# A hybrid retention and RG-LRU block: row factors squared earlier in the first steps, and all weight sums and rotary adds on VectorE

## The chip, the cores and the metric

The kernel runs on one core of a Trainium2 chip. The metric is the device time of one execution in microseconds (us); of the kernel before, three runs gave 929.69 us as the median (928.82 to 929.72). All arithmetic is float32; a product is split into high and low parts of the type fp32r and takes three matmuls.

The engines are named as in the profile: PE is TensorE, PEld its weight loads, DVE VectorE, ACT ScalarE, POOL GpSimd, SP the engine that issues most loads. Each engine executes its own instructions in order.

## The reference

One layer over 528 tokens (16 meta tokens ahead of 512) of width 1024:

```python
u = rmsnorm(h, mix_norm_w)
q, k, v, g_ret, lru_in, lru_gate, gate_a, gate_b = split(u @ w_in)      # 8 times 1024 columns
q, k = rotary(q), rotary(k) * 128 ** -0.5                               # 8 heads of 128
o = normed(chunk_retention(q, k, v))                                    # chunks of 128
y_ret = (silu(g_ret) * o) @ w_branch_ret
r = rg_lru(causal_depthwise_conv(lru_in))
y_lru = (gelu(lru_gate) * r) @ w_branch_lru
h = h + (sigmoid(gate_a) * y_ret + sigmoid(gate_b) * y_lru) @ w_out
u = rmsnorm(h, ffn_norm_w); g, up = split(u @ w_ffn_in)                 # 2 times 2816 columns
h = h + (silu(g) * up) @ w_ffn_out
out = rmsnorm(h, final_norm_w)[16:]
```

## The kernel before

The weights come in slabs of 2048 columns per partition, each in four quarters (`a21`, `a22`, `a11`, `a12`) of 128x512, loaded by SP into eight buffers (`raw`). `emit` (L268) prepares a quarter: ACT casts it to its high part (`hi`, L295), DVE subtracts that for the low part (`lo`, L299). A ring of nine high and low parts lies ahead of TensorE, and `weights` prepares up to eight pieces beyond the one asked for.

A slab is multiplied in one of two ways. `plain` (L439) uses the four quarters as they are. `fast` (L382) does with seven products what takes eight: it needs four sums of quarters (`s1` to `s4`, by `combine`, L260), sums of activations (`sums_of`, L531), and some adds of the products. Inside `fast`, DVE adds two products (`pz`, L398) after the first four blocks; the next block of TensorE writes the bank that this add reads, so TensorE can't go on before it. Of `w_in`, 13 slabs are fast, among them queries 0 to 3, keys 2, gates and LRU inputs; half of the values (`w_v`) is fast as well. Where `SUMS_ON_POOL` names the weights, `combine` puts the sums on POOL; for the FFN's `w_fi` they are on DVE. The queries and keys then go through `rotate` (L707): ACT copies halves, DVE multiplies by the tables (L720 or L716, and L721), POOL adds (L722).

The program order after the first steps is the order of the source, with other work deferred behind a count of TensorE time (`defer`, `tick`): retention, the convolution, the recurrence. The compiler's planner sets the order of each engine from it by a timeline of its own. The first steps are different: `first_steps` (L847) runs the list `FIRST_STEPS` (L47) in a section whose order on PE, DVE, ACT and POOL is kept as written; the planner may put later instructions between.

In that list, `f`, `h`, `l` weigh and split a token tile of 128 rows (first digit) and half of the width (second digit); `H` and `L` split a quarter of the value weights; `v` goes on with `plain_values` (L792) to the products of the next step: the first half of the width for tiles 0 and 1, the second half for tiles 0 and 1, then tile 2 (here called the third products), and, in a step behind the list, tile 3 (the fourth). `q` (`row_factor`, L593) squares a token tile's rows with a sum on ACT (L599), raises the mean to -0.5 on POOL (L602, L603) and puts the factor on a diagonal (L605). For tiles 2 and 3, `T` (`halve`) transposes the rows on TensorE by that diagonal into the bank `uT`; `x`, `h`, `l` weigh and split the result. For tiles 0 and 1 and the meta rows, whose transposed rows are loaded, `b` (`across`, L607) spreads the factors over all partitions by a product with ones, into the bank `rb`. `um` (`norm_meta`, L643) normalises the meta rows with DVE and ACT. `e01` evicts the products of tiles 0 and 1 from their banks, and `n`, `g`, `j` scale and split those tiles with the spread factors.

Of the kernel before, what the change touches and what calls it, by code (L numbers as in the profile page):

```python
# [14 lines left out]
ALU = mybir.AluOpType  # L15
# [29 lines left out]


FIRST_STEPS = ("f01 h01 H l01 L f00 H h00 L l00 H L H L v f11 h11 f10 h10 l11 l10 v H L H L H L H L v "  # L47
               "q2 qm q3 T21 T20 x21 h21 l21 x20 h20 l20 v q0 q1 T31 T30 bm b0 b1 x31 h31 l31 x30 h30 l30 um v "
               "e01 n00 g00 n01 g01 j00 j01 n10 g10 n11 g11 j10 j11").split()
STAGES = (3.5, 3.5, 9.0)  # L50
OUT = 14.0
BEGIN = 11.0
# [1 line left out]
LAST_K = 4  # L54

ON_POOL = {"w_out": (1, 3)}
SUMS_ON_POOL = ("w_in", "w_v")
Z_POOL = False
C_POOL = ()
STEPS = (2.0, 2.0, 1.0, 2.0)  # L60
# [51 lines left out]
class Slots:  # L112
# [12 lines left out]
    def get(self, n=SEQ, dt=F32):  # L125
        if n <= T and dt == F32:
            if self.halves:
                slot, i = self.halves.pop(0)
            else:
                slot, i = [*self.open(dt), 0], 0  # L130
                self.halves.append((slot, 1))
            slot[2] += 1
            t = slot[1][:, i * T:i * T + n]
            self.held[id(t)] = (t, slot, i)
        else:
            tag, mem = self.open(dt)
            t = mem[:, :n]
            self.held[id(t)] = (t, tag, None)
        return t

    def put(self, *tiles):
        for t in tiles:
            _, slot, i = self.held.pop(id(t))
            if i is None:
                self.free.append(slot)
                continue
            slot[2] -= 1
            self.halves.append((slot, i))
            if slot[2] == 0:
                self.halves = [h for h in self.halves if h[0] is not slot]  # L150
                self.free.append(slot[0])
# [3 lines left out]
def hybrid_block(ctx: ExitStack, tc: tile.TileContext, a: dict):  # L155
    nc = tc.nc
# [42 lines left out]
    for step in PLAN.split():  # L199
# [5 lines left out]
        else:  # L205
            key, base = SLAB_OF[step[0]]
# [7 lines left out]
    def on_pool(key, i, c):  # L214
        return c in ON_POOL.get(key, ())
# [23 lines left out]
    state = {"n": 0, "look": 0}  # L239

    def behind(ins, other):

        if other is not None:
            tc.add_manual_dep(ins.ins, other.ins.name, mybir.DependencyInfo(
                mybir.DependencyClass.NoSync, mybir.DependencyReason.DATA), reason="issue order")
        return ins
# [4 lines left out]
    sums = {}  # L251

    def quarter(key, i, c, queue=None):

        if (key, i, c) not in raws:
            raws[key, i, c] = wpool.tile([P, Q4], F32, tag="raw", bufs=RAW, name=f"raw_{key}{i}_{c}")
            (queue or nc.sync).dma_start(raws[key, i, c], a[key][i][:, c * Q4:(c + 1) * Q4])
        return raws[key, i, c]

    def combine(key, i, name, x, y, op):  # L260
        sums[key, i, name] = wpool.tile([P, Q4], F32, tag="sum", bufs=SUMS, name=f"{name}_{key}{i}")
        if key in SUMS_ON_POOL:
            behind(nc.gpsimd.tensor_tensor(sums[key, i, name], x, y, op=op), state.get("diag"))
        else:
            nc.vector.tensor_tensor(sums[key, i, name], x, y, op=op)
        return sums[key, i, name]

    def emit(n, later=False):  # L268
        key, i, c = pieces[n]
        a21, a22, a11, a12 = (lambda q=q: quarter(key, i, q) for q in range(4))  # L270
        apart = key == "w_v"
        if apart and c == "s1":
            t = kept[key, i] = sums[key, i, "s1"] = get()
            nc.gpsimd.tensor_tensor(t, a21(), a22(), op=ALU.add)
        elif apart and c == "s3":
            combine(key, i, "s3", a11(), a21(), ALU.subtract)
        elif apart and c in ("s2", "s4"):
            t = kept[key, i]
            if (key, i, "s2") not in sums:
                sums[key, i, "s2"] = t  # L280
                nc.gpsimd.tensor_tensor(t, t, a11(), op=ALU.subtract)
            if c == "s4":
                combine(key, i, "s4", a12(), t, ALU.subtract)
        elif c == "s1":
            s1 = combine(key, i, "s1", a21(), a22(), ALU.add)
            combine(key, i, "s3", a11(), a21(), ALU.subtract)
            s2 = combine(key, i, "s2", s1, a11(), ALU.subtract)
            combine(key, i, "s4", a12(), s2, ALU.subtract)
        if c in ("s1", "s2", "s3", "s4"):
            src = sums[key, i, c]  # L290
        else:
            src = quarter(key, i, {"a21": 0, "a22": 1, "a11": 2, "a12": 3}.get(c, c))
        hi = wpool.tile([P, Q4], F32R, tag="hi", bufs=RING, name=f"hi{n}")
        lo = wpool.tile([P, Q4], F32R, tag="lo", bufs=RING, name=f"lo{n}")
        nc.scalar.copy(hi, src)  # L295
        loaded[pieces[n]] = hi, lo

        def low(engine):
            engine.tensor_tensor(lo, src, hi.bitcast(F32), op=ALU.subtract)  # L299

        if later:
            return low
        low(nc.gpsimd if on_pool(key, i, c) else nc.vector)
        if (key, i) in kept and (key, i, "s4") in sums and {(key, i, "s2"), (key, i, "s4")} <= set(pieces[:n + 1]):
            put(kept.pop((key, i)))

    def advance(name):

        first = pieces.index(name)
        while state["n"] < min(first + RING, len(pieces)):  # L310
            emit(state["n"])
            state["n"] += 1

    def weights(*names):

        first, last = pieces.index(names[0]), pieces.index(names[-1])
        while state["n"] < min(max(last + state["look"], first) + 1, first + RING, len(pieces)):
            emit(state["n"])
            state["n"] += 1
        return [loaded.pop(n) for n in names]  # L320
# [231 lines left out]
    for load in FIRST_LOADS.split():  # L552
        t = int(load[1:] or 0)
        if load[0] == "w":
            key, i, c = pieces[t]
# [151 lines left out]
    def rotate(x, n, banks=()):  # L707

        tmp = get(4 * n)
        t = tmp.rearrange("p (j n t) -> p j n t", j=2, n=2)  # L710
        table = lambda r: rope[:, r, :, :n].unsqueeze(1).broadcast_to([P, 2, 2, n])
        for j, hs, pb in banks:
            pb = pb.rearrange("p (h t) -> p h t", t=n)
            nc.scalar.copy(t[:64, j, hs], pb[64:])
            nc.scalar.copy(t[64:, j, hs], pb[:64])
            nc.vector.tensor_tensor(x[:, j, hs], pb, rope[:, 0, hs, :n], op=ALU.mult)  # L716
        if not banks:
            nc.scalar.copy(t[:64], x[64:])
            nc.scalar.copy(t[64:], x[:64])
            nc.vector.tensor_tensor(x, x, table(0), op=ALU.mult)  # L720
        nc.vector.tensor_tensor(t, t, table(1), op=ALU.mult)  # L721
        nc.gpsimd.tensor_tensor(x, x, t, op=ALU.add)  # L722
        put(tmp)

    def value_block(out, w, x, h, start, tiles=(0, 1)):
# [121 lines left out]
    def first_steps(v):  # L847
        lows, parts = [], {}
        for step in FIRST_STEPS:
            kind, t, c = step[0], step[1:2], step[2:3]  # L850
            if step in ("v", "e01"):
                next(v, None)
            elif kind == "H":
                lows.append(emit(state["n"], True))
                state["n"] += 1
            elif kind == "L":
                lows.pop(0)(nc.vector)
            elif step == "um":
                norm_meta()
            elif kind == "q":  # L860
                row_factor(t if t == "m" else int(t))
            elif kind == "T":
                halve(int(t), int(c))
            elif kind == "x" or kind in "hl" and int(t) > 1:
                next(halves[int(t), int(c)], None)
            elif kind == "b":
                across(t if t == "m" else int(t))
            else:
                t, c = int(t), int(c)
                if kind == "n":  # L870
                    parts[t, c] = scaled(t, c)
                elif kind == "g":
                    nc.scalar.copy(parts[t, c][1][0], parts[t, c][0])
                elif kind == "j":
                    f, (hi, lo) = parts.pop((t, c))
                    nc.vector.tensor_tensor(lo, f, hi.bitcast(F32), op=ALU.subtract)
                else:
                    {"f": weighted, "h": raw_high, "l": raw_low}[kind](t, c)
# [362 lines left out]
    for hf in range(2):  # L1241
# [4 lines left out]
        for t, i in steps:  # L1246
# [5 lines left out]
            if i == KT - 1:  # L1252
                y = h_sb[t][:, hf * 512:(hf + 1) * 512]
# [191 lines left out]
```

## Time and profile before

| | us |
|---|---|
| median of three runs | 929.69 |
| the profiled execution | 928.09 |
| its span | 926.3 |
| PE busy | 907.6 |
| DVE busy | 659.3 |
| ACT busy | 462.6 |
| POOL busy | 177.3 |

The span runs from the first to the last instruction of the program; 1.8 us of the execution lie outside. Busy times are sums over an engine; TensorE's ends are modelled, and its matmuls overlap by a part. A row of a group gives line, engine, operation, output and inputs, shape and count, then busy us and mean ns, then the idle time ahead of it and what ended it. A row of a timeline gives start and duration in us; a row of a stretch gives its length and each engine's busy time in it.

### The profile page before, as it was taken

Reading aid. Unit: us, or ns where it says so; the run is one execution under the profiler, and the core shown is the slowest. Engines: PE = TensorE matmul, PEld = TensorE weight load, DVE = VectorE, ACT = ScalarE, POOL = GpSimd, SP = SyncE. Lnnn points to the kernel's source line nnn. Section 1 sums busy time; section 2 is a strip of 40 time slices with the busy share of each in tenths; the row PEclk is TensorE's granted clock in tenths of the full one; section 3 lists DMA queues with packets and bytes.
Section 4 is the critical chain, followed back from the end, with each engine's and each line's share of the span. In section 5 each row is a group of like instructions: output and inputs, shape, how many; then the busy total and the mean of one; then the engine's idle time right before and its main releaser. Section 6 shows DMA issues by size and latency. Waiting matters only on the chain.

```text
span 926.3 us, 16867 instructions
## 1 busy us (share of the span) xinstructions
PE 907.6 (98%) x6572; PEld 855.2 (92%) x6572; DVE 659.3 (71%) x1014; ACT 462.6 (50%) x815; POOL 177.3 (19%) x149
## 2 busy tenths in 40 slices
PE   8999999999999999999999999999999999999996
PEld 7899999999999889999998888999999999888885
DVE  5898986997788836787744536969999998832222
ACT  5654544653555337747932315545556566632213
POOL 2344553455351002112100212000000000000003
PEclk9999999999999999999999999999999999999999
DMA  9222122141133332232442222223333233432202
GB/s 327 80 95 91 58 81 92 58 126 46 60 111 115 110 100 76 91 109 88 148 136 91 93 91 76 81 79 120 104 106 120 96 123 96 151 111 91 80 1 91
DMA packets 49071, 92.59 MB, mean 100 GB/s; under 512 B 5584, under 2 KB 5840, under 8 KB 48992
## 3 DMA queue, kind: packets, MB, share of 16 engines
q1 hardware_dynamic: 47408, 87.55, 29.2%
q10 hardware_dynamic: 1584, 3.97, 1.3%
q8 instruction: 51, 0.84, 0.4%
q14 instruction: 28, 0.23, 0.1%
HBM read 89.40 MB, written 2.10 MB: 99 GB/s over the span
## 4 chain that ended last, share of the span: by engine, by line
PE 85%; DVE 3%; issue 1%; ACT 0%; POOLq 0%; POOL 0%; DVEq 0%
PE fo L369 4%; PE fo L368 4%; PE fo L367 4%; PE zwf L378 4%; PE zwf L377 4%; PE zwf L379 4%; PE yxf L378 3%; PE yxf L379 3%; PE yxf L377 3%; PE lg L377 2%; PE gate L377 2%; PE gate L379 2%; PE lg L379 2%; PE gate L378 2%; PE lg L378 2%; PE wo L367 2%
## 5 line engine op out<-in xcount | busy, mean ns | idle before, releaser
L299 DVE TENSOR_TENSOR lo<-raw_w_in,hi 128x512 fp32r<-128x512 f32 x99 | 85.2, 867 | 29.8 <-ACT hi L295 29.6
L295 ACT CAST hi<-raw_w_in 128x512 fp32r<-128x512 f32 x99 | 60.8, 619 | 62.7 <-PE w_br L368 13.9
L378 PE MATMUL zwf<-b,hi 128*128 128x256 f32 x304 | 84.7, 279 | 0.0
L379 PE MATMUL zwf<-b,lo 128*128 128x256 f32 x304 | 84.6, 278 | 0.0
L377 PE MATMUL zwf<-b,hi 128*128 128x256 f32 x304 | 84.5, 279 | 0.0
L299 DVE TENSOR_TENSOR lo<-raw_w_fo,hi 128x512 fp32r<-128x512 f32 x44 | 30.1, 690 | 63.3 <-ACT hi L295 63.3
L295 ACT CAST hi<-s_w_fi 128x512 fp32r<-128x512 f32 x76 | 47.2, 623 | 44.5 <-PE zwf L378 36.0
L368 PE MATMUL fo<-lo,b 128*128 128x512 f32 x176 | 69.3, 394 | 0.0
L367 PE MATMUL fo<-hi,b 128*128 128x512 f32 x176 | 69.3, 394 | 0.0
L369 PE MATMUL fo<-hi,b 128*128 128x512 f32 x176 | 69.3, 395 | 0.0
L1330 POOL TENSOR_TENSOR b<-b,b 128x512 f32<-128x512 f32 x4 | 5.1, 1287 | 330.0 <-ACT b L1329 330.0
L378 PE MATMUL yxf<-b,hi 128*128 128x256 f32 x228 | 62.8, 279 | 0.0
L379 PE MATMUL yxf<-b,lo 128*128 128x256 f32 x228 | 62.7, 278 | 0.0
L295 ACT CAST hi<-raw_w_fo 128x512 fp32r<-128x512 f32 x44 | 27.3, 620 | 70.2 <-PE fo L369 64.6
L295 ACT CAST hi<-raw_w_fi 128x512 fp32r<-128x512 f32 x69 | 42.3, 621 | 39.0 <-PE yxf L378 13.9
L377 PE MATMUL yxf<-b,hi 128*128 128x256 f32 x228 | 61.0, 278 | 0.0
L299 DVE TENSOR_TENSOR lo<-s_w_fi,hi 128x512 fp32r<-128x512 f32 x76 | 51.2, 688 | 11.9 <-ACT hi L295 10.1
L299 DVE TENSOR_TENSOR lo<-s_w_in,hi 128x512 fp32r<-128x512 f32 x52 | 49.2, 947 | 14.1 <-ACT hi L295 13.1
L378 PEld LDWEIGHTS zwf<-b,hi 128*128 128x128 f32 x304 | 57.1, 188 | 0.0
L377 PEld LDWEIGHTS zwf<-b,hi 128*128 128x128 f32 x304 | 57.1, 188 | 0.0
L379 PEld LDWEIGHTS zwf<-b,lo 128*128 128x128 f32 x304 | 57.1, 188 | 0.0
L299 DVE TENSOR_TENSOR lo<-raw_w_fi,hi 128x512 fp32r<-128x512 f32 x69 | 47.0, 687 | 5.9 <-ACT hi L295 5.8
(422 smaller groups left out, 3242.6 us busy)
## 6 DMA issues: line engine op xcount, KB each, us to landing
raw_w_in<-in_w_in SPq DMA_DIRECT2D x112, 256.0 KB, 3.1
raw_w_fi<-in_w_fi SPq DMA_DIRECT2D x88, 256.0 KB, 3.2
raw_w_fo<-in_w_fo SPq DMA_DIRECT2D x44, 256.0 KB, 3.0
raw_w_br<-in_w_br SPq DMA_DIRECT2D x16, 256.0 KB, 3.1
raw_w_bl<-in_w_bl SPq DMA_DIRECT2D x16, 256.0 KB, 3.1
raw_w_out<-in_w_out SPq DMA_DIRECT2D x16, 256.0 KB, 2.9
raw_w_v<-in_w_v SPq DMA_DIRECT2D x15, 256.0 KB, 3.4
b<-in_x SPq DMA_DIRECT2D x4, 512.0 KB, 6.9
```

What stands on the lines that cost most here:

```text
L295: nc.scalar.copy(hi, src)
L299: engine.tensor_tensor(lo, src, hi.bitcast(F32), op=ALU.subtract)
L367: nc.tensor.matmul(out, wh, xh, start=start, stop=False, skip_group_check=True)
L368: nc.tensor.matmul(out, wh, xl, start=False, stop=False, skip_group_check=True)
L369: nc.tensor.matmul(out, wl, xh, start=False, stop=stop, skip_group_check=True)
L377: nc.tensor.matmul(out, wh, xh, start=start and i == 0, stop=False, skip_group_check=True)
L378: nc.tensor.matmul(out, wh, xl, start=False, stop=False, skip_group_check=True)
L379: nc.tensor.matmul(out, wl, xh, start=False, stop=i == 3, skip_group_check=True)
L1330: nc.gpsimd.tensor_tensor(y[:, done], y[:, done], wfin[:, done], op=ALU.mult)
```

## The change

Two things. In `FIRST_STEPS` the row factors of tiles 0 and 1 (`q0 q1`) are made right behind those of the other tiles, ahead of the splits of tile 2, where they stood behind them; `b0 b1` stand behind the third products, where they stood ahead; `um` stands between the two splits of tile 3's second half. And all sums of weights for `w_in` and `w_v`, and the last add of `rotate`, go from POOL to DVE; `SUMS_ON_POOL` is gone, and with it the edge that kept these sums behind the diagonals.

```diff
-               "q2 qm q3 T21 T20 x21 h21 l21 x20 h20 l20 v q0 q1 T31 T30 bm b0 b1 x31 h31 l31 x30 h30 l30 um v "
-               "e01 n00 g00 n01 g01 j00 j01 n10 g10 n11 g11 j10 j11").split()
+               "q2 qm q3 q0 q1 T21 T20 x21 h21 l21 x20 h20 l20 v T31 T30 bm x31 h31 um l31 x30 h30 l30 v "
+               "b0 b1 e01 n00 g00 n01 g01 j00 j01 n10 g10 n11 g11 j10 j11").split()
...
-SUMS_ON_POOL = ("w_in", "w_v")
...
-        if key in SUMS_ON_POOL:
-            behind(nc.gpsimd.tensor_tensor(sums[key, i, name], x, y, op=op), state.get("diag"))
-        else:
-            nc.vector.tensor_tensor(sums[key, i, name], x, y, op=op)
+        nc.vector.tensor_tensor(sums[key, i, name], x, y, op=op)
...
-            nc.gpsimd.tensor_tensor(t, a21(), a22(), op=ALU.add)
+            nc.vector.tensor_tensor(t, a21(), a22(), op=ALU.add)
...
-                nc.gpsimd.tensor_tensor(t, t, a11(), op=ALU.subtract)
+                nc.vector.tensor_tensor(t, t, a11(), op=ALU.subtract)
...
-        nc.gpsimd.tensor_tensor(x, x, t, op=ALU.add)
+        nc.vector.tensor_tensor(x, x, t, op=ALU.add)
```

## The prediction

> **What bounds the kernel now.** I read the page's busy times first, then what TensorE waits for, then the stretches around those waits, and only there the single engines.
>
> ```profile
> span 926.3 us, 16867 instructions
> PE 907.6 (98%) x6572; PEld 855.2 (92%) x6572; DVE 659.3 (71%) x1014; ACT 462.6 (50%) x815; POOL 177.3 (19%) x149
> ```
>
> TensorE is busy for 98% of the span, so no more than 18.7 us of idling (926.3 - 907.6) is there to be won, and the start before the first load cannot be. TensorE's longest waits behind the start (us in total, times, longest):
>
> ```profile
> ...
> PE zwq L377 <- DVE pzq L398: 2.5, 2, 1.9
> PE rb L615 <- POOL b L605: 1.9, 2, 1.6
> PE o L1000 <- DVE b L992: 1.8, 3, 1.0
> ...
> ```
>
> The wait of `rb` (the spread row factors) belongs to the first part of the edit, those on DVE to the second. The stretches around them (columns: length; busy time and count of PE, PEld, DVE, ACT, POOL; granted clock; DMA share; GB/s):
>
> ```profile
> 24.80:28.00 3.20, 1.27 (x8) 0.92 (x7) 1.80 (x3) 1.29 (x4) 2.83 (x6) 0.97 0.20 75
> 28.00:31.30 3.30, 3.30 (x17) 3.30 (x17) 2.74 (x5) 0.58 (x4) 3.30 (x3) 0.52 0.00 0
> 31.30:44.60 13.30, 13.30 (x116) 13.00 (x114) 13.09 (x24) 9.85 (x19) 1.83 (x2) 1.00 0.17 56
> 44.60:63.40 18.80, 18.80 (x158) 18.80 (x156) 18.80 (x21) 12.14 (x24) 9.10 (x5) 1.00 0.32 104
> 63.40:65.50 2.10, 0.23 (x3) 0.03 (x1) 2.10 (x3) 0.00 (x0) 1.17 (x1) 1.00 0.32 114
> 87.70:90.10 2.40, 1.08 (x8) 0.67 (x6) 2.35 (x9) 0.89 (x2) 0.00 (x0) 1.00 0.30 96
> 116.10:119.10 3.00, 1.83 (x15) 1.44 (x13) 2.97 (x7) 0.00 (x0) 2.92 (x3) 1.00 0.02 5
> 210.60:211.60 1.00, 0.38 (x4) 0.16 (x2) 1.00 (x3) 0.00 (x0) 1.00 (x2) 1.00 0.00 0
> 285.00:600.00 315.00, 315.00 (x2097) 289.49 (x2096) 205.58 (x295) 160.31 (x260) 40.33 (x30) 1.00 0.32 100
> ```
>
> TensorE starves at 25, 63, 88, 116 and 211 us. From 31 us on DVE has hardly a free moment until 65 us, so there it is the second bound. After the stall at 25 us the granted clock is 0.52 for 3.3 us. From 285 us on nothing is missing; the moved instructions all lie before, so that part only shifts.
>
> **The order of the first steps.** TensorE, ACT and POOL around 25 us:
>
> ```profile
> 17.84 0.18 ACT L599 ACTIVATION_READ_ACCUMULATOR b<-b 128x1 f32 x1
> 20.27 0.62 ACT L516 CAST b<-b 128x512 fp32r<-128x512 f32 x1 [2.25 <-DVE b L513]
> 22.79 1.05 ACT L599 ACTIVATE b<-b 128x1024 f32<-128x1024 f32 x1
> 27.01 0.61 POOL L605 TENSOR_SCALAR b<-ident,rx 128x128 f32<-128x128 f32 x1
> 24.86 0.39 PE L615 MATMUL rb<-b,ones 16*128 16x16 f32 x2
> 25.62 0.49 PE L615 MATMUL rb<-b,ones 128*128 128x128 f32 x2 [0.37 <-POOL b L605]
> 27.67 0.71 PE L615 MATMUL rb<-b,ones 128*128 128x128 f32 x2 [1.56 <-POOL b L605]
> 28.03 0.56 PE L367 MATMUL v<-hi,b 128*128 128x256 f32 x1
> 22.91 0.69 DVE L518 TENSOR_TENSOR b<-b,b 128x512 fp32r<-128x512 f32 x1
> ```
>
> The last of the two squares runs until about 25 us (22.79 plus two of 1.05 us), POOL's diagonal for tile 1 ends at 27.62, `b1` waits for it, and the third tile's products stand behind `b1` on TensorE's queue although they do not read it: their last operand, the low part of tile 2, was written by 23.60. In the new order they follow `bm` directly, at about 25.1 (24.86 and a quarter of a microsecond) in place of 28.03: **-2.9 us**. The two squares move into the 2.25 us that ACT has free from 18.02 to 20.27: they need 2 x 1.05 = 2.1 us, so the split behind them is late by a tenth at most. If tile 1's rows came a microsecond later than that, the split would be late by as much, still inside the 1.5 us between 23.60 and 25.1. POOL's small instructions for both factors end 2.6 us behind the squares now (27.62 against 25.0), so they are done by about 23 then, and nothing asks for them before the third products end.
>
> The cold clock: 15 products of 256 columns take 28.03 to 31.31. At full clock the 116 matmuls of the next stretch take 13.30 us, 0.115 us each, so 15 take 1.7: **-1.5 us** if the clock stays up. `b0` and `b1` themselves are not gone, they follow the third products: four matmuls, 28.03 - 27.67 = 0.36 us for two, so **+0.6 us** with the gaps. Together **-3.8 us** at the fourth tile's products.
>
> The Trainium skill (TensorE: Matmul & The Clock Gate, Part 1, "What's actually happening") lets the clock fall after an idle window of about 3.4 us. Here the clock fell to 0.52 after a stretch of 3.2 us in which TensorE was still busy for 1.27; the measurement decides, so I count the cold clock as caused by this stall. Read strictly, the rule would leave the 1.5 us in place; that is rival four.
>
> **The sums go to VectorE.** What is moved, and what the same work costs on DVE in the FFN, where it already runs there:
>
> ```profile
> L263 POOL TENSOR_TENSOR s_w_in<-raw_w_in,raw_w_in 128x512 f32<-128x512 f32 x26 | 38.8, 1498 | 52.3 <-DMA raw_w_in<-in_w_in 34.5 <-DVE lo L299 17.7
> L722 POOL TENSOR_TENSOR b<-b,b 128x1056 f32<-128x1056 f32 x4 | 10.9, 2732 | 8.5 <-DVE b L721 7.2 <-DVE rr_o L1009 1.3
> L265 DVE TENSOR_TENSOR s_w_fi<-raw_w_fi,raw_w_fi 128x512 f32<-128x512 f32 x38 | 26.0, 689 | 1.6 <-DMA raw_w_fi<-in_w_fi 1.0
> L299 DVE TENSOR_TENSOR lo<-s_w_fi,hi 128x512 fp32r<-128x512 f32 x76 | 51.2, 688 | 11.9 <-ACT hi L295 10.1
> L299 DVE TENSOR_TENSOR lo<-raw_w_in,hi 128x512 fp32r<-128x512 f32 x99 | 85.2, 867 | 29.8 <-ACT hi L295 29.6
> L299 DVE TENSOR_TENSOR lo<-s_w_in,hi 128x512 fp32r<-128x512 f32 x52 | 49.2, 947 | 14.1 <-ACT hi L295 13.1
> 13.35 2.49 DVE L299 TENSOR_TENSOR lo<-raw_w_v,hi 128x512 fp32r<-128x512 f32 x4
> ```
>
> DVE gets 13 slabs of four sums for `w_in`, eight for `w_v`, and eight rotary adds of 1024 or 1056 columns. Four subtractions in a row take 2.49 us, so one more in a full queue costs 0.60 us ((2.49 - 0.69) / 3), and a rotary add about 1.2 (twice the columns): 60 x 0.60 + 8 x 1.2 = **+46 us** of DVE work. Against it, the same subtraction takes 688 ns where POOL is silent and 867 or 947 ns where POOL adds: 99 x 0.179 + 52 x 0.259 = **-31 us** on these two groups alone. So DVE's total changes little, and what counts is where. Up to the stall at 63 us:
>
> ```profile
> 27.58 1.73 POOL L263 TENSOR_TENSOR s_w_in<-raw_w_in,raw_w_in 128x512 f32<-128x512 f32 x1
> 28.10 1.36 DVE L646 TENSOR_TENSOR mt<-mt,vec 128x128 f32<-128x128 f32 x1
> 29.57 0.29 DVE L648 TENSOR_TENSOR um<-mt,rb 128x128 f32<-128x128 f32 x1
> 31.98 1.27 DVE L653 COPY b<-um 128x32 f32<-128x32 f32 x1
> 33.27 0.17 DVE L653 COPY b<-um 128x32 f32<-128x32 f32 x1
> 50.33 1.26 DVE L541 TENSOR_TENSOR b<-b,b 128x1056 fp32r<-128x1056 f32 x1
> 53.04 2.01 DVE L541 TENSOR_TENSOR b<-b,b 128x1056 fp32r<-128x1056 f32 x1
> 61.59 3.53 DVE L299 TENSOR_TENSOR lo<-raw_w_in,hi 128x512 fp32r<-128x512 f32 x2
> 65.05 0.41 DVE L398 TENSOR_TENSOR pzq<-zwq,wsq 128x256 f32<-128x256 f32 x1
> ```
>
> Beside POOL's adds, 128 columns take 1.36 us and not 0.29, 32 columns 1.27 and not 0.17, 1056 columns 2.01 and not 1.26, two subtractions 3.53 and not 1.29 (2 x 0.60 + 0.09). These four alone are 1.07 + 1.10 + 0.75 + 2.24 = 5.2 us; three subtractions at 55 to 60 us and two steps of the meta rows in the same two stretches of POOL work add, by my estimate from the 867 and 947 above and these ratios, 1 to 3.7: 6.2 to 8.9 us leave DVE's queue before the `pzq` of 65.05. Two slabs of sums and one rotary add come in: 8 x 0.60 + 1.2 = 6.0. The queue gets 0.2 to 2.9 us shorter, and the meta rows, put ahead of `l31`, can fill up to 1.4 us in which DVE is idle between 24.80 and 28.00 (1.80 of 3.20 busy). So `pzq` comes 0.2 to 4.3 us sooner, at 60.7 to 64.9. I take 3.6, nearer the upper end, because the pair of 3.53 us directly ahead of `pzq` is measured and not estimated. TensorE reaches this point 3.8 us sooner and waits about as long as before: **-3.6 us stand at 65 us**, and not -3.8 with the wait gone.
>
> The stalls at 88, 116 to 119 and 211 us sum to 1.3 + 1.2 + 0.6 = 3.1 us of idling by the rows above. They are waits on DVE, which gains there as much as it gets; but a long operation in front of the awaited one gets shorter, and POOL's add of 2.7 us in front of the retention becomes 1.2. Bounds: all 3.1 gone, or 2 us more where a sum now stands ahead of an awaited operation (three sums of 0.60). I take two thirds of the gain, **-2.1 us**, nearer to the FFN, where DVE carries all sums and TensorE waits for none.
>
> Sum: -3.6 - 2.1 = **-5.7 us**. The profiled execution took 928.09 us (span 926.3 and 1.8 around it), which gives 922.4. The median of the runs, 929.69, is 1.6 above it, so I forecast **924.0 us**, on its own between 921.5 and 926.5.
>
> **The rivals.**
> 1. *Contention was all of it.* With POOL silent, every wait on DVE goes: 3.8 + 1.9 (63 us: 2.10 less 0.23) + 3.1 = 8.8: 920.9. For it speaks the FFN, which runs without gaps; against it that DVE was full from 31 to 65 us.
> 2. *DVE gives it back.* `pzq` gains only its lower 0.2 to 1.5 us, TensorE arrives 3.8 us sooner and waits 4 to 5 us at 60; the stretch at 25 us shows that such a hole halves the clock for 3.3 us, another 1.5. Gain 0 to 1.5: 929.0. For it: the 44.60:63.40 row, DVE 18.80 of 18.80. Against: the 3.53 us pair directly ahead of `pzq`.
> 3. *Slower: a sum waits for its load at the head of DVE's queue.* POOL's first sums wait 34.5 us for loads; on POOL nobody stands behind them, on DVE the splits and `pz` do. One load takes 3.1 us from issue to landing (the row below), and the prefetch hides it until it is late. There are 15 slabs or pairs; a loss begins from the third late load (3 x 3.1 = 9.3 against 5.7), and four cost 12.4 - 5.7 = +6.7: 936.4. Against it: 38 sums of the FFN wait 1.6 us in all.
>
> ```profile
> raw_w_in<-in_w_in SPq DMA_DIRECT2D x112, 256.0 KB, 3.1
> ```
>
> 4. *The cold clock stays* because it was not the stall that caused it: 924.0 + 1.5 = 925.5.
> 5. *The reorder doesn't free TensorE*: the third products still wait, now for the low part of tile 2, because tile 1's rows hold up ACT. 924.0 + 3.8 = 927.8.
>
> **How the numbers follow.** Forecast 0.50; rival one 0.16, two 0.13, three 0.10, four 0.06, five 0.05. The range 919.6 to 929.4 holds the forecast, four, five, most of one (0.03 lies below it) and half of two, and leaves out three: 0.19 in all. A measurement of this kernel can tell about 0.2%, or 1.9 us, from no change: faster below 927.8, slower above 931.6. Faster: 0.50 + 0.16 + 0.06 + half of five 0.02 + 0.03 of two = 0.77. Same: the other 0.03 of five and 0.09 of two = 0.12. Slower: rival three and 0.01 of two = 0.11.
>
> **What would show it.** Right: TensorE's waits without `rb`, the third products right behind `bm` near 25 us, a granted clock of 1.00 from 28 to 31 us; POOL busy under 75 us (177.3 less the 109 us of the moved groups); the split of `raw_w_in` at 0.69 us; DVE's total within 15 us of 659. Wrong: a `zwq` wait on `pzq` of over 3 us, sums of DVE idle behind a load of `raw_w_in`, a clock below 1.00 anywhere between 31 and 900 us, or new waits of TensorE between 120 and 290 us.

## The result, and the profile after

The changed kernel takes **918.17 us** (median of four runs, 918.10 to 918.47) against 929.64 us of the kernel before beside it (928.82 to 929.72): a ratio of 0.9879, 95% interval 0.9862 to 0.9896. That is 11.5 us faster, about twice the 5.7 us forecast, and 1.4 us below the predicted range.

The first lines of the changed kernel's page, and TensorE's waits (us in total, times, longest):

```profile
span 916.4 us, 16814 instructions
...
PE 904.4 (99%) x6572; PEld 854.1 (93%) x6572; DVE 657.7 (72%) x1082; ACT 463.2 (51%) x815; POOL 71.4 (8%) x81
...
```

```profile
PE warm L186 <- POOL ident masks.py:199: 2.9, 1, 2.9
PE yxq L373 <- ACT pzq L395: 0.9, 1, 0.9
PE v L363 <- ACT b L582: 0.4, 1, 0.4
PE v L364 <- DVE lo L295: 0.3, 1, 0.3
PE v L365 <- DVE b L587: 0.2, 1, 0.2
```

Of the three long waits of before, on `rb`, on `pzq` by DVE and on `o`, none is left. Behind the start there is one new wait, of 0.9 us, on ACT. (Lines have moved up by up to four: L299 is L295 here, L398 is L394, L722 is L718.) The stretches that answer to those shown of before (length; busy time and count of PE, PEld, DVE, ACT, POOL; granted clock; DMA share; GB/s):

```profile
18.00:24.40 6.40, 6.40 (x59) 6.28 (x57) 4.04 (x7) 3.73 (x8) 5.50 (x11) 1.00 1.03 380
24.40:30.90 6.50, 6.50 (x56) 6.47 (x55) 5.84 (x19) 3.35 (x10) 0.49 (x1) 1.00 0.24 79
...
40.40:52.10 11.70, 11.70 (x98) 11.70 (x97) 11.70 (x17) 8.41 (x15) 0.00 (x0) 1.00 0.29 91
52.10:67.00 14.90, 14.90 (x128) 14.90 (x127) 12.32 (x20) 7.41 (x14) 0.00 (x0) 1.00 0.33 107
...
182.00:183.30 1.30, 0.44 (x4) 0.24 (x3) 1.30 (x3) 0.93 (x3) 0.00 (x0) 1.00 0.71 254
```

In the stretches from 18.00 to 67.00 us TensorE is busy all of the time at a granted clock of 1.00. DVE is still full from 40 to 52 us (11.70 of 11.70), and from 52 to 67 us it now has 2.6 us free (12.32 of 14.90), where before it had hardly any from 31 to 65 us. The first steps, from the timeline:

```profile
18.86 1.06 ACT L595 ACTIVATE b<-b 128x1024 f32<-128x1024 f32 x1
19.92 0.60 ACT L512 CAST b<-b 128x512 fp32r<-128x512 f32 x1
24.16 0.73 POOL L601 TENSOR_SCALAR b<-ident,rx 128x128 f32<-128x128 f32 x1
24.40 0.39 PE L611 MATMUL rb<-b,ones 16*128 16x16 f32 x2
24.72 0.39 PE L363 MATMUL v<-hi,b 128*128 128x256 f32 x1
```

The third products follow `bm` at 24.72, in place of 28.03. The last square ends as the split behind it begins, at 19.92. DVE around the `pzq` that TensorE waited for before, the first product of TensorE that needs it, and the groups that the change touched:

```profile
58.28 0.68 DVE L295 TENSOR_TENSOR lo<-raw_w_in,hi 128x512 fp32r<-128x512 f32 x1
58.89 0.41 DVE L394 TENSOR_TENSOR pzq<-zwq,wsq 128x256 f32<-128x256 f32 x1
59.22 1.28 DVE L295 TENSOR_TENSOR lo<-s_w_in,hi 128x512 fp32r<-128x512 f32 x2
60.42 1.24 DVE L718 TENSOR_TENSOR b<-b,b 128x1056 f32<-128x1056 f32 x1
...
64.10 0.28 PE L373 MATMUL zwq<-b,hi 128*128 128x256 f32 x1
```

```profile
L295 DVE TENSOR_TENSOR lo<-raw_w_in,hi 128x512 fp32r<-128x512 f32 x99 | 70.4, 718 | 29.8 <-ACT hi L291 29.6
L295 DVE TENSOR_TENSOR lo<-s_w_in,hi 128x512 fp32r<-128x512 f32 x52 | 35.5, 687 | 11.3 <-ACT hi L291 11.1
L261 DVE TENSOR_TENSOR s_w_in<-raw_w_in,raw_w_in 128x512 f32<-128x512 f32 x26 | 17.7, 685 | 0.6 <-DMA raw_w_in<-in_w_in 0.3
```

`pzq` comes at 58.89, 6.2 us sooner than the 65.05 of before, and TensorE needs it only at 64.10, where it needed it from 63.6 on before. Two splits in a row take 1.28 us and not 3.53. DVE does 68 more instructions (1082 against 1014) in 1.6 us less (657.7 against 659.3). Its moved sums wait for loads for 2.5 us in all, 2.2 of them those of `w_v` and 0.3 those of `w_in`, and no wait of TensorE follows from it.

### The profile page after: what moved, and what is told of

It reads as the page before. It is cut to its first block, busy times and chain, and to the rows that moved or that the text cites. A ratio compares the mean times of both kernels' runs of the same rounds, so it can differ in the third digit from the quotient of the medians.

```text
span 916.4 us, 16814 instructions
## 1 busy us (share of the span) xinstructions
PE 904.4 (99%) x6572; PEld 854.1 (93%) x6572; DVE 657.7 (72%) x1082; ACT 463.2 (51%) x815; POOL 71.4 (8%) x81
## 4 chain that ended last, share of the span: by engine, by line
PE 79%; DVE 0%; issue 0%; POOLq 0%; POOL 0%; ACT 0%
PE fo L363 4%; PE fo L365 4%; PE fo L364 4%; PE zwf L375 4%; PE zwf L373 4%; PE zwf L374 4%; PE yxf L374 3%; PE yxf L375 3%; PE yxf L373 3%; PE gate L373 2%; PE lg L373 2%; PE lg L375 2%; PE gate L375 2%; PE gate L374 2%; PE lg L374 2%; PE wo L363 2%
## 5 line engine op out<-in xcount | busy, mean ns | idle before, releaser
L295 DVE TENSOR_TENSOR lo<-raw_w_in,hi 128x512 fp32r<-128x512 f32 x99 | 70.4, 718 | 29.8 <-ACT hi L291 29.6
L295 DVE TENSOR_TENSOR lo<-raw_w_fo,hi 128x512 fp32r<-128x512 f32 x44 | 30.1, 689 | 63.0 <-ACT hi L291 63.0
L295 DVE TENSOR_TENSOR lo<-s_w_fi,hi 128x512 fp32r<-128x512 f32 x76 | 52.0, 687 | 12.2 <-ACT hi L291 10.4
L291 ACT CAST hi<-s_w_in 128x512 fp32r<-128x512 f32 x52 | 32.3, 620 | 40.4 <-PE zwgate L374 9.2
L295 DVE TENSOR_TENSOR lo<-raw_w_fi,hi 128x512 fp32r<-128x512 f32 x69 | 47.0, 687 | 6.0 <-ACT hi L291 5.9
L295 DVE TENSOR_TENSOR lo<-s_w_in,hi 128x512 fp32r<-128x512 f32 x52 | 35.5, 687 | 11.3 <-ACT hi L291 11.1
```

## The experiments

The theory at this point was that DVE lost its time to POOL, and that both of the edit's halves need each other. The rivals: one half did it alone; the clock did it; the moved work merely runs faster on DVE. The comparisons below are against the kernel before in the same series, unless another is named.

### The order alone, and the sums alone

The kernel before with the new list of steps, sums and rotary adds still on POOL:

```diff
-               "q2 qm q3 T21 T20 x21 h21 l21 x20 h20 l20 v q0 q1 T31 T30 bm b0 b1 x31 h31 l31 x30 h30 l30 um v "
-               "e01 n00 ...
+               "q2 qm q3 q0 q1 T21 T20 x21 h21 l21 x20 h20 l20 v T31 T30 bm x31 h31 um l31 x30 h30 l30 v "
+               "b0 b1 e01 n00 ...
```

> The new order of the first steps alone; sums and rotary adds stay on POOL. Theory A (the two parts add, and DVE's slow-down beside POOL is the second): the wait of rb and the half clock go, key slab 0 starts 4.2 us sooner as in the changed kernel, and the waits on DVE at 63 to 211 us stay, so 925.4 us (924.4 to 926.6). Rival B (DVE gives the gain back while POOL is still adding): a wait on pzq of 4 us or more, 928 to 929.6. Rival C (the order was all of it): under 920.

Measured: 926.72 us, ratio 0.9973 (0.9962 to 0.9984). TensorE's longest wait, a stretch and the timeline of this kernel:

```profile
PE zwq L377 <- DVE pzq L398: 3.2, 1, 3.2
```

```profile
64.80:68.20 3.40, 2.88 (x13) 2.88 (x14) 2.43 (x7) 0.13 (x1) 0.00 (x0) 0.50 0.25 82
```

```profile
61.68 2.70 POOL L722 TENSOR_TENSOR b<-b,b 128x1056 f32<-128x1056 f32 x1 [4.34 <-DVE b L721]
...
61.43 3.49 DVE L299 TENSOR_TENSOR lo<-raw_w_in,hi 128x512 fp32r<-128x512 f32 x2
64.85 0.41 DVE L398 TENSOR_TENSOR pzq<-zwq,wsq 128x256 f32<-128x256 f32 x1
```

The wait on `rb` is gone, but `pzq` still comes at 64.85: POOL's rotary add stretches the two splits ahead of `pzq` to 3.49 us. TensorE arrives sooner and waits 3.2 us in place of 1.9, and the clock is halved behind it. So a part of the gain is given back at `pzq`; what stays is 2.3 us, more than rival B's 0 to 1.6 and 0.1 us outside theory A's range.

The other half alone: the changed kernel with the old list of steps.

```diff
-... q3 q0 q1 T21 ... v T31 T30 bm x31 h31 um l31 x30 h30 l30 v b0 b1 e01 ...
+... q3 T21 ... v q0 q1 T31 T30 bm b0 b1 x31 h31 l31 x30 h30 l30 um v e01 ...
```

> The sums and rotary adds on DVE, the first steps in the old order. Theory A: the wait of rb on POOL and the half clock from 28 to 31 us are there as before, the waits on DVE are gone, so 929.6 less 7.3 (11.5 less 4.2) = 922.3 us (921.3 to 923.5). Rival B (the parts need each other): 925 or more. Rival C (the order was all of it): 929.

Measured: 923.70 us, ratio 0.9943 (0.9928 to 0.9957). Its waits, and the timeline at the diagonals:

```profile
PE rb L611 <- POOL b L601: 3.3, 2, 2.9
```

```profile
27.48 1.67 POOL L601 TENSOR_SCALAR b<-ident,rx 128x128 f32<-128x128 f32 x1
...
29.20 0.80 PE L611 MATMUL rb<-b,ones 128*128 128x128 f32 x2 [2.91 <-POOL b L601]
```

All waits on DVE behind the first steps are gone, but the one on `rb` got longer (3.3 us in place of 1.9), since POOL's diagonal of tile 1 took 1.67 us beside DVE's sums and not 0.61. The clock is at 0.50 behind it, from 28.9 to 32.2 us. The parts alone are worth 2.3 and 5.3 us, together 11.5: each half alone makes the wait longer that the other half clears. The 923.70 us are 0.2 above theory A's range.

### POOL's work as the cause

The changed kernel, in which POOL does every sum of `w_in` and `w_v` once more, into a tile that nobody reads. No instruction of TensorE, DVE or ACT in its trace waits for one of these adds; three loads do, as the adds read their buffers. TensorE's order differs from the changed kernel's in 42 of 6572 places.

```diff
-        nc.vector.tensor_tensor(sums[key, i, name], x, y, op=op)
+        nc.vector.tensor_tensor(sums[key, i, name], x, y, op=op)
+        if key in ("w_in", "w_v"):
+            unread = wpool.tile([P, Q4], F32, tag="unread", bufs=2)
+            nc.gpsimd.tensor_tensor(unread, x, y, op=op)
```

> The changed kernel, and POOL computes every weight sum of w_in and w_v once more into a tile that nobody reads; DVE keeps its own sums. Theory A (POOL's adds slow DVE's two-input operations): the split of raw_w_in takes 0.85 us or more in place of 0.72, TensorE waits on DVE again, 922 to 928 us, since DVE now carries the sums and the slow-down. Rival D (before, TensorE waited because POOL delivered sums and rotary adds late): nobody waits for POOL here, so 918.2 to 919.

Measured: 940.51 us, ratio 1.0139 (1.0113 to 1.0165), so 22 us above the changed kernel for work that no result depends on, and far above the 922 to 928 expected. Its longest waits behind the start, and three groups:

```profile
PE oT L942 <- DVE b L1006: 4.3, 1, 4.3
PE s L975 <- DVE b L718: 3.8, 1, 3.8
```

```profile
L295 DVE TENSOR_TENSOR lo<-raw_w_in,hi 128x512 fp32r<-128x512 f32 x99 | 76.0, 775 | 26.4 <-ACT hi L291 26.3
L295 DVE TENSOR_TENSOR lo<-s_w_in,hi 128x512 fp32r<-128x512 f32 x52 | 43.5, 845 | 2.6 <-ACT hi L291 2.4
L261 POOL TENSOR_TENSOR unread_s_w_in<-raw_w_in,raw_w_in 128x512 f32<-128x512 f32 x26 | 46.0, 1787 | 30.6 <-DMA raw_w_in<-in_w_in 30.6
```

The splits of sums take 845 ns and not 687; those of `raw_w_in` take 775 and not 718, less than the 850 expected. TensorE waits for DVE again, in new places, and behind four of the waits (at 61, 85, 143 and 218 us) the clock is at 0.50 for 3.4 us, which costs some 1.7 us each. That POOL's adds slow DVE, and that this reaches TensorE, is shown.

The same with a copy in place of the add: POOL reads one input of each sum.

```diff
+            nc.gpsimd.tensor_copy(unread, x)
```

> The changed kernel, and POOL copies the first input of every weight sum of w_in and w_v into a tile that nobody reads (one input where the unread adds had two). Theory J (any POOL work of this size slows DVE's two-input operations): the split of raw_w_in at 0.76 us or more, and 921 us or more. Rival K (only POOL's two-input operations do): the split stays at 0.72 us, 918.2 to 919.

Measured: 918.74 us, ratio 0.9892 (0.9876 to 0.9907), as good as the changed kernel. Groups and timeline:

```profile
L295 DVE TENSOR_TENSOR lo<-s_w_in,hi 128x512 fp32r<-128x512 f32 x52 | 35.7, 692 | 8.7 <-ACT hi L291 8.5
```

```profile
41.27 10.00 POOL L261 COPY unread_s_w_in<-raw_w_in 128x512 f32<-128x512 f32 x2 [13.04 <-DMA raw_w_in<-in_w_in]
51.22 1.07 POOL L261 COPY unread_s_w_in<-s_w_in 128x512 f32<-128x512 f32 x1
...
50.72 1.09 DVE L295 TENSOR_TENSOR lo<-s_w_in,hi 128x512 fp32r<-128x512 f32 x1
```

The time is the one that rival K names, but its reason, that one-input work of POOL leaves DVE alone, doesn't hold: a split beside a copy took 1.09 us, 0.4 more than its 0.68. Two copies took 10.00 us while DVE ran one operation after another. So it is not POOL's presence that counts but how long one of its instructions holds DVE up: about 0.4 us for this copy, 2.2 us for the rotary add (3.53 less 1.28).

### Which of POOL's jobs

The changed kernel with the rotary adds back on POOL:

```diff
-        nc.vector.tensor_tensor(x, x, t, op=ALU.add)
+        nc.gpsimd.tensor_tensor(x, x, t, op=ALU.add)
```

> The changed kernel with the eight rotary adds back on POOL. Theory A (contention counts by the length of POOL's adds beside two-input operations of DVE): eight adds of 2.7 us slow DVE by up to 2 us each where it is full, at 60 and near 110 us, and one or two waits of TensorE on DVE return: 919 to 922. Rival I (only the sums counted): 918.2 to 918.7.

Measured: 924.65 us, ratio 0.9949 (0.9932 to 0.9967), more than the 919 to 922 expected. A wait, a stretch behind it and the timeline:

```profile
PE o L996 <- DVE b L988: 3.8, 2, 2.5
```

```profile
114.20:117.50 3.30, 3.30 (x17) 3.30 (x17) 2.89 (x8) 0.82 (x3) 0.00 (x0) 0.50 0.05 13
```

```profile
57.22 4.52 POOL L718 TENSOR_TENSOR b<-b,b 128x1056 f32<-128x1056 f32 x1 [31.77 <-DVE b L717]
...
57.56 1.25 DVE L537 TENSOR_TENSOR b<-b,b 128x1056 fp32r<-128x1056 f32 x1
58.73 0.68 DVE L295 TENSOR_TENSOR lo<-raw_w_in,hi 128x512 fp32r<-128x512 f32 x1
59.33 0.42 DVE L394 TENSOR_TENSOR pzq<-zwq,wsq 128x256 f32<-128x256 f32 x1
59.66 3.23 DVE L295 TENSOR_TENSOR lo<-s_w_in,hi 128x512 fp32r<-128x512 f32 x2
```

Eight adds cost some 6 us: TensorE waits 4.5 us for DVE in the retention (`o`, with two smaller waits of 0.7 us), and behind the longest wait a half-clock stretch costs 1.7. The rows show how POOL holds DVE up: POOL's add is issued at 57.22, but three DVE operations up to 59.66 keep their usual durations; then the pair takes 3.23, 1.95 more than 1.28, and POOL ends at 61.74.

The reverse: the new order, the rotary adds on DVE, the sums of `w_in` and `w_v` on POOL as before.

```diff
+SUMS_ON_POOL = ("w_in", "w_v")
...
-        nc.vector.tensor_tensor(sums[key, i, name], x, y, op=op)
+        if key in SUMS_ON_POOL:
+            behind(nc.gpsimd.tensor_tensor(sums[key, i, name], x, y, op=op), state.get("diag"))
+        else:
+            nc.vector.tensor_tensor(sums[key, i, name], x, y, op=op)
```

> The new order and the rotary adds on DVE, the weight sums on POOL. Theory A: 60 adds of 1.4 us beside DVE keep most of the slow-down (the split of raw_w_in over 0.80 us), and the wait on pzq near 60 us stays in part: 922 to 926. Rival I' (the long rotary add ahead of pzq was the cause): 918 to 920.

Measured: 923.27 us, ratio 0.9935 (0.9918 to 0.9953). The waits of this kernel:

```profile
PE o L1000 <- DVE b L992: 2.1, 1, 2.1
PE zwq L377 <- DVE pzq L398: 1.1, 1, 1.1
```

With both on POOL and the new order it is 926.72, with the rotary adds alone there 924.65, with the sums alone there 923.27, with neither 918.17 (in three series): eight rotary adds cost some 6.5 us and 60 sums some 5.1. Here too the clock is at 0.50 behind the wait on `o`, from 113.4 to 116.7 us.

### The clock of the kernel before

The kernel before once more, for a second profile.

> The kernel before, unchanged, profiled once more, because its profiled execution (928.09) lay 1.6 us under its median. Theory E (the clock falls a second time in most executions, after the stall at 63 us): a profile of about 929.6 shows two stretches of half clock. Rival F: one stretch as before, and the 1.6 us lie in longer waits.

Measured: 929.72 us; the span is 927.9 and not 926.3. Three stretches of this profile:

```profile
28.90:32.40 3.50, 3.50 (x19) 3.50 (x18) 2.94 (x5) 1.60 (x7) 3.42 (x4) 0.52 0.15 44
63.60:66.60 3.00, 1.12 (x9) 1.02 (x9) 3.00 (x6) 0.00 (x0) 1.05 (x1) 1.00 0.31 94
66.60:69.95 3.35, 3.35 (x18) 3.35 (x17) 0.99 (x2) 0.62 (x1) 0.00 (x0) 0.50 0.22 72
```

In the first profile of before the clock fell once ahead of the last microseconds, here twice: the hole at 63 us is followed by a second stretch at half clock. At a clock of 0.50 the 3.35 us do the work of 1.7, so about 1.7 are lost; the two spans differ by 1.6, and so did the profiled execution (928.09) and the median (929.69). The changed kernel has neither hole, and its profiled execution is its median.

### Which half of the reorder

`b0 b1` back ahead of the third products, the squares early; then the squares late, `b0 b1` behind:

```diff
-... q3 q0 q1 T21 ... v T31 T30 bm x31 h31 um l31 x30 h30 l30 v b0 b1 e01 ...
+... q3 q0 q1 T21 ... v T31 T30 bm b0 b1 x31 h31 um l31 x30 h30 l30 v e01 ...
```

> The changed kernel with b0 b1 put back ahead of the third products; the squares stay early. Theory G (either move alone frees the third products): POOL's last diagonal ended at 24.89 us in the changed kernel, so b1 waits 0.3 us at most, and the time is 918.2 to 919. Rival H (the products have to stand ahead of b1): a wait of rb of 1.5 us or more, and with the half clock 921 to 922.5.

```diff
-... q3 q0 q1 T21 ... v T31 T30 bm ...
+... q3 T21 ... v q0 q1 T31 T30 bm ...
```

> The changed kernel with q0 q1 put back behind the split of tile 2; b0 b1 stay behind the third products. TensorE's and VectorE's orders are those of the changed kernel, ACT's differs in two places. Theory G: the diagonals are done by 29.2 us at the latest (as in the kernel with the old order), ahead of b0 at 30.5, so no wait: 918.0 to 919. Rival H' (the squares must be early): the split of tile 3 comes 2 us later on ACT, the fourth products wait: 920 or more.

Measured: 918.71 (ratio 0.9888, 0.9873 to 0.9903) and 917.53 (0.9875, 0.986 to 0.9889). Neither has a wait on `rb`, and the third products start at 25.46 and 24.77 us. Either move alone frees TensorE; the other adds nothing. The late squares lie below their expected range of 918.0 to 919.

### The new wait, and the changed kernel again

The wait of 0.9 us at 182, on the timeline of the changed kernel:

```profile
182.37 0.62 ACT L291 CAST hi<-raw_w_in 128x512 fp32r<-128x512 f32 x1 [0.81 <-PE yxq L374]
...
182.89 0.37 ACT L395 COPY pzq<-yxq 128x256 f32<-128x256 f32 x1
...
183.31 0.39 PE L373 MATMUL yxq<-b,hi 128*128 128x256 f32 x1 [0.87 <-ACT pzq L395]
```

A cast waits for TensorE to give its buffer free, and the copy that TensorE needs next is queued behind the cast. An edge (an order between two instructions that the program adds) puts the copy first, in the slab of queries 3 alone; it ran beside the changed kernel again, and beside a version with both this edge and the late squares.

```diff
-        nc.scalar.copy(hi, src)
+        behind(nc.scalar.copy(hi, src), state.get("pz"))
...
-        nc.scalar.copy(pz[:, 0, :n], x)
+        copied = nc.scalar.copy(pz[:, 0, :n], x)
+        state["pz"] = copied if (key, s) == ("w_in", Q + 3) else None
```

> The changed kernel with one more edge: in the slab of queries 3, ACT's copy of the product x (line 395) goes ahead of the cast that stood before it and waited for a free buffer of the ring. Theory L: TensorE's last wait of 0.87 us on that copy goes, 917.3 us (0.9 less than the changed kernel in the same call). Rival M: the cast behind it is late by as much and the wait moves, 918.2.

> The changed kernel unchanged, to stand beside the others of this call: 917.5 to 918.7 us, one stretch of full clock from about 7 us to the end, and the wait of 0.9 us near 182 us.

> The edge of queries 3, and the squares of tiles 0 and 1 back behind the split of tile 2 (0.6 us less than the changed kernel when it ran alone, in another call). If both count: 916.7 us; if the 0.6 us were the call's, 917.3.

Measured: the edge 918.21 us (917.81 to 918.44), the changed kernel 918.59 (918.52 to 919.07), both edits **917.34** (917.04 to 917.46; ratio to before 0.9874, 0.9859 to 0.9889). The edge brings 0.4 us of the 0.9 expected, as the wait falls from 0.9 to 0.5; with the late squares it is 1.25 us, and the two ranges don't meet. That is the lowest median of all versions; the late squares alone, in another series, come within 0.2 us of it.

### Why the late squares are faster: where the tiles lie

The late squares leave every wait as it is, yet the FFN's seven-product stretch, from the first product of `zwf` to the first of `fo`, is 1.5 us shorter. It takes 180.9 us in the kernel before as well, and 182.45 in all kernels above with the early squares. TensorE's order there is the same in all of them. What differs is that early diagonals open one more slot of SBUF (the memory on the chip, which the program cuts into slots that its tiles take and give back), so that the list of free slots is another one from there on. First the twelve activation tiles of the FFN were put into the other kernel's slots, by sorting the free list ahead of them, in both directions, and once with the edge on the copy:

```diff
+    slots.free.sort(key=...)        # a fixed list of 24 slots
     h_sb = [get(D) for t in range(NC_)]
```

> The changed kernel with the free slots sorted once ahead of the output rows, so that the twelve tiles with the FFN's activations lie in the same slots as in the kernel with the squares late; TensorE's order is untouched. In seven kernels with the squares early the seven-product slabs of the FFN took 182.45 us from their first to the last stage's first matmul, in four with the squares late (or in the old place) 180.92. Theory N (the slots in which the operands lie set it): 180.9 and 916.9 us. Rival O (something else of the early squares): 182.4 and 918.4.

> The kernel with the squares late, and the free slots sorted so that eleven of those twelve tiles lie in slots that the changed kernel uses for them, most of them at the same place in the list. Theory N: the FFN stretch goes from 180.92 to 182.4 us, 919.0 us. Rival O: 180.92, 917.5.

> The sorted slots on the changed kernel, and the edge that puts the copy of product x first in the slab of queries 3. Theory N and L together: 918.4 less 1.5 less 0.4 = 916.5 us; by rival O 918.0.

Measured: 920.10, 920.46 and 919.45 us, all slower than either parent, and the FFN stretch takes 183.6, 183.5 and 183.6 us. Neither theory expected that. It wasn't a clean test: the eight tiles of sums, made later, then lay in a third arrangement, neither parent's. So all 214 slots from the first sums on were written down as a list, and each kernel got the other's:

```diff
-        tag = self.free.pop(0)
+        tag = SLOT_PLAN.get(self.n, self.free[0])
+        self.free.remove(tag)
```

> The changed kernel, with every slot of SBUF from the first sums of activations on handed out as in the kernel with the late squares (the list of 214 slots is written into Slots.open; the order of the program is the changed kernel's). The earlier attempt put only twelve activation tiles of the FFN into the other kernel's slots, and the eight tiles of sums still lay elsewhere. Placement theory: all places now being those of the late squares, the FFN's seven-product stretch takes 180.9 us in place of 182.45, and the whole about 917.4. Rival (the early squares themselves, or the order of the splits, set the pace): 182.4 us and about 918.6, as before. If it is 183 or more, as in the two kernels with sorted slots, neither holds.

> The other way round: the changed kernel with the late squares, and every slot from the first sums on handed out as in the changed kernel. Placement theory: the FFN's seven-product stretch goes from 180.9 to 182.45 us, the whole to about 918.7. Rival: it stays at 180.9 us and about 917.5.

Measured: the changed kernel with the slots of the late squares 917.54 us (917.25 to 917.65; ratio 0.9875, 0.9855 to 0.9895), the late squares with the changed kernel's slots 919.88 (919.57 to 919.96; 0.99, 0.9876 to 0.9924). The FFN stretch of the changed kernel, and of the one with the other slots, each up to the same product:

```profile
600.10:782.50 182.40, 182.40 (x1562) 182.40 (x1561) 167.15 (x271) 108.06 (x206) 0.00 (x0) 1.00 0.34 109
```

```profile
600.90:781.80 180.90, 180.90 (x1562) 180.90 (x1562) 166.18 (x271) 108.05 (x206) 0.00 (x0) 1.00 0.34 110
```

The same 1562 recorded matmuls in the same order, at full clock, take 1.5 us less for nothing but the slots: PE, DVE, ACT and POOL run the same instructions in the same order in both traces. The reverse gives 182.9 us where 182.45 was expected, so it goes the right way and a little too far. That the slots set this pace is shown. Which of them, and why, is not: the trace shows products 113 to 114 ns apart in some blocks and 118 in others, and what the fast blocks have in common stays open.

The slots also work the other way ahead of this stretch. From the branch to the FFN it is 314.8 us in the changed kernel, and 315.4 with the late squares' slots, as in the kernel before. On the whole the changed kernel's slots cost 1.05 us (918.59, when it ran again, against 917.54 in another series).

## Why the prediction was wrong, and where it was right

The balance in spans, from the starts of TensorE's stages in the two traces (926.3 - 916.4 = 9.9 us):

| | predicted | measured |
|---|---|---|
| up to the fourth tile's end (keys 0 start at 44.60, then 40.37) | -3.8 | -4.2, of which 0.46 was there at 18 us |
| from there to the branch (295.53, then 285.31) | +0.2 - 2.1 = -1.9 | -6.0 |
| to the FFN (610.94, then 600.11) | 0 | -0.6 |
| the seven-product stretch of the FFN | 0 | +1.5 |
| to the end | 0 | -0.6 |
| second half-clock stretch, not in the profiled execution | 0 | -1.6 |

**The start was right.** Third products 28.03 to 24.72 is -3.3, less 0.46 that was there already at 18 us: -2.85 where -2.9 was predicted. (That point varies between executions: it is at 18.00 and 18.29 us in the two profiles of the changed kernel.) The clock stays at 1.00 (-1.5), `b0 b1` follow. Rivals four and five fell with that. That the clock fell because of the hole is borne out by all profiles: in the three with the hole near 25 to 29 us (two of before, one of the sums alone) the clock falls behind it, in the other sixteen it doesn't. One reading was off at no cost: POOL's last diagonal ended at 24.89 and not by about 23, well ahead of `b0` at 30.53.

The Trainium skill (TensorE: Matmul & The Clock Gate, Part 1, "What's actually happening") says the activity window of about 3.4 us runs freely, and lets the clock fall after an idle one. The free-running window fits the two profiles of before, in which the same hole at 63 us is followed by a drop once and once not. A whole idle window was not needed here: TensorE's longest idle time in the hole was 1.9 us, it was busy for 1.12 of 3.00 us, and the half clock then lasted 3.35 us.

**The step that failed** is "TensorE reaches this point 3.8 us sooner and waits about as long as before: -3.6 us stand at 65 us, and not -3.8 with the wait gone". `pzq` came 6.2 us sooner, beyond the bound of 4.3, and the wait of 1.9 us went altogether. (The sentence has a slip as well: with the wait gone it would be -3.8 - 1.9 = -5.7, as rival one counts.)

The queues of DVE ahead of `pzq` hold the same operations in both traces, but for what was moved, so the error can be taken apart. These operations got 9.44 us shorter, a little more than the 6.2 to 8.9 predicted: the three subtractions at 55 to 60 us alone had lost 2.6 us beside POOL (they took 1.77, 1.44 and 1.44 us, not 0.68). Eight sums brought 4.89 us and not 6.0, because the planner put the rotary add behind `pzq` (60.42). The idle time of DVE shrank by 1.15 us of the 1.4 allowed, and 0.46 were there at the start. 9.44 - 4.89 + 1.15 + 0.46 = 6.16. In the old order TensorE would have come to the guarded product at about 59.2, as `pzq` ended (59.30). The planner did more: it put 41 other products ahead, so that TensorE needs `pzq` only at 64.10. By these rows either alone would have ended this wait, or all but 0.1 us of it; no run parts the two, and the prediction had neither.

The same error sits in "I take two thirds of the gain, -2.1 us". All the later stalls went, and they were larger than the 3.1 us read from three stretches, as busy times hold the modelled ends of matmuls. By the starts of the matmuls, each against the median distance of its shape, TensorE lost 2.2 us from 60 to 70 us, and 5.1 from 70 to 130 and 205 to 220 us; in the changed kernel it loses 0.3 there in all. Against it stands 1.1 us more around the new wait at 182: 2.2 + 5.1 - 0.3 - 1.1 = 5.9 of the 6.0. That new wait is also a sign of being wrong from the prediction's list, and the only one that came, but for the 0.3 us of sums behind loads of `raw_w_in`.

The third term that failed is the 1.6 us between the profiled execution and the median, which the prediction carried along as a constant. It was a half-clock stretch behind one of the stalls to be removed (the second profile of before shows it), and it went with the stall. So the 5.8 us by which the forecast fell short are 4.1 between keys 0 and the branch, 1.6 in this offset, and 0.1 net of the other rows.

So **rival one, "Contention was all of it", is what happened**; it had 0.16. "Against it that DVE was full from 31 to 65 us" was the misjudged evidence: much of that time DVE was slowed, and with the sums added to the same work it is through 6 us sooner. The unread adds show it from the other side. Rival one's 920.9 is still 2.7 us too slow, since two things are in no case: the 1.6 us of the second half-clock stretch, and 1.1 us net of larger stalls, the new wait and the slots (9.9 in spans against 8.8).

**Rival two** describes the reorder alone in kind (2.3 us, with a 3.2-us wait on `pzq`), and is wrong beside the moved sums. **Rival three** fell: the moved sums wait 2.5 us for loads in all, and TensorE doesn't wait for it. POOL's 71.4 us (under 75) and DVE's total (657.7, within 15 of 659) were as said; the split of `raw_w_in` took 718 ns where 690 was named.

**What no step had**: slots. The earlier diagonals open one more, and the FFN, 600 us later, pays 1.5 us of the gain back; the -0.6 just before the FFN goes with the slots as well. The -0.6 at the end is not explained.

## What to carry to other kernels

Where two engines slow each other, read the durations of single instructions beside each other, not the group's mean, and count the engine as loaded by the work that it would have alone. Look for half-clock stretches behind each stall, also where the profiled execution has none: a gap between it and the median can be one, and goes with the stall. Two edits that clear waits one behind the other are tried together before either is judged. Where a planner sets the order, ask which wait it will move away, and not only which one gets shorter. An order that opens one buffer more can change the pace of a stage far behind it.

## What the hardware showed that was not expected

POOL and DVE did not share: they took turns by whole instructions. In the kernel with the rotary add on POOL, the add stood for 4.52 us, 2.4 of them while DVE's operations ran at their usual pace, and then DVE's pair lost 1.95 us; two copies on POOL stood for 10.00 us beside a full DVE. The Trainium skill (SBUF — State Buffer, "SBUF: two separate sides") calls the port that the two share an exclusive lock, held for a whole instruction by whichever starts first. These rows agree with it. What a DVE operation loses goes with the length of POOL's instruction and is somewhat less: 0.4 us beside a copy that takes 0.61 us where DVE is idle, 1.1 us beside a sum (two inputs of 128x512 take POOL 1.29 us where DVE is idle), 1.95 to 2.25 us beside a rotary add, which takes 2.7 us.

The place of tiles in SBUF moved TensorE's pace with nothing else changed: 180.9, 182.4, 182.9 and 183.5 to 183.6 us for the same recorded matmuls under five sets of slots.
